# Expert loop of an mLSTM, differential-attention and mixture-of-experts layer: which waits the load queue holds, how tokens beyond 128 are interlaced, and the shape of the mask product

## The chip, the cores and the metric

The kernel runs on one core of one Trainium2 chip. The metric is the device time of one execution in microseconds; the time of a kernel is the median of several executions.

## The reference

One layer over 2048 tokens of width 1024, all in float32. Cut to what matters here:

```python
h = rms_norm(x, norm1_w)
x = x + hybrid_mixer(h, ...)           # mLSTM heads and differential attention, one output projection
h = rms_norm(x, norm2_w)
...
# differential attention: a block of 128 queries sees the keys of its own and earlier chunks of 64
mask = key_chunk[None, :] <= q_chunk[:, None]
p = jax.nn.softmax(jnp.where(mask, s, -jnp.inf), axis=-1)
attn = p[:, :, 0] - lam * p[:, :, 1]
...
# mixture of experts: top 1 of 4 groups, top 2 of its 8 experts, 32 experts in all
hid = jax.nn.silu(xb @ w_gate[e]) * (xb @ w_up[e])     # 1024 -> 512
return hid @ w_down[e]                                 # 512 -> 1024
...
x = x + sum over the 2 experts of weight * expert(h)
```

The routing depends on the inputs. Worked out from the reference with its inputs, 20 of the 32 experts get at most 128 tokens, 6 get 129 to 160, 4 get 161 to 192, and 2 get more (201 and 241).

## The kernel before

The program has four stages, one after the other: the projection of 16 blocks of 128 tokens (to about 320 us of the profiled span), attention and mLSTM for 4 heads (to about 1165 us), output projection with routing (to about 1395 us), and the expert loop (to the end).

**Attention stage.** One loop goes over 64 blocks (head, 128 queries) and writes the atoms of several streams into one order; `score` (L560 on) multiplies queries by keys in float32r, and on the diagonal chunk adds a third product into the same PSUM tile, L577: `qm` by `km`, both bfloat16 with one partition (1 x 128), whose product is -1e30 where the later chunk of 64 is hidden. There are 64 blocks and 2 maps, so 128 mask products.

**Expert loop (L1321).** The places 0 to 32 of the loop run over the experts in an order that the device works out itself: experts 0 and 1 first, then the experts with more than HEAVY tokens (`t3`, L1134) spread evenly between the others, with LEAD moving them earlier or later in their share. For each place:

- The first 128 tokens: gather their rows (`gather`, POOL), transpose and split them into a high and a low part (`turn`), `ffn1` for d = 0..7 (L1227, 6 float32r products of 512 columns for each d), tanh and gating (`hidden`), transpose (`turn_h`, L1232), `ffn2` for f = 0..3 (L1242, 6 products each, one `down(f)`), scale (`emit`, L1247, ACT) and add into the output by a scatter (`scatter`, L1251, POOL). `ffn2` of a place runs in the next place's iteration, and its scatter in the one after that.
- The weights: an expert has 6 raw tiles of 128 x 2048 float32 (1 MiB): 4 with gate and up (L847, two loads of 512 KB), 2 with down (L850). A ring of 12 raw tiles `R` holds two experts. Each half tile is split by ACT (`H`, L66) and DVE (`L`, L70); `ready` puts these splits 6 halves ahead of their use, into the same order as all other work of ACT and DVE.
- Tokens 128 and on (`few`, L1291): if an expert has more than 128, a pass of 32 tokens, if more than 160 a second pass of 32, if more than 192 one of 64. A pass transposes its rows (`few_turn_x`, copy by ACT), multiplies them by the RAW tiles (L1272, then L1287, in plain float32, in column groups of 32 or 64), and writes to `yE`; then one scatter returns all 128 rows of `yE`. So a raw tile is free only when the passes of its expert are over, and the plain path must wait for the branch in any case, as the release stands behind it.

**The load queue.** SP issues everything in the order of the program. In an iteration: `fetch_slots(e + 3)` (L1185: 4 KB of slots into one of 5 buffers `ix`; the buffer is that of place e - 2, whose scatter, issued in this same iteration, must have landed), then behind the branch `done(e - 1, 4)` and `done(e - 1, 5)` (w_down of place e + 1), `done(e, 0)` to `done(e, 3)` (gate and up of place e + 2):

```python
fetch_slots(e + AHEAD)
...
few(e, Q, 0, (lambda: down(2), lambda: down(3)))
with tc.If(n > P + Q, label=f"more{e}b", preferred_fallthrough_block=True):
    few(e, Q, Q)
    with tc.If(n > P + M, label=f"more{e}c", preferred_fallthrough_block=True):
        few(e, M, M)
scatter(yE, IX[e][:, 1])
...
for j in (4, 5):
    done(e - 1, j)
for j in range(4):
    done(e, j)
```

## Time and profile before

| | |
|---|---|
| time, median of 3 runs | 2278.57 us (2271.84 to 2289.45) |
| the profiled execution: time, span | 2281.88 us, 2279.8 us |
| mean granted TensorE clock | 0.969 |
| busy in the span: PE, DVE, ACT, POOL | 92%, 70%, 54%, 23% |
| HBM read and written | 378.51 MB, 87.65 MB |

PE is the matmul engine, DVE VectorE, ACT ScalarE, POOL GpSimd, SP the queue that issues loads. Busy times are those of one profiled execution. Matmuls are pipelined and their ends are modelled, so the distance between the starts of two matmuls says more than the length of one. A wait is put down to the instruction whose semaphore came last.

### The profile page before, as it was taken

The page shows a single profiled execution, that of the slowest core. Times are in us where ns is not written, and L with a number is a line of the kernel's source. Part 1 is how long each engine was busy: PE and PEld are TensorE (multiplying, and loading weights), DVE is VectorE, ACT ScalarE, POOL GpSimd, SP SyncE. Part 2 cuts the span into 40 slices and gives each one's busy share as a digit, 9 for nine tenths or more (in the row PEclk, how much of TensorE's full clock was granted, in tenths as well). Part 3 has the DMA queues.
Part 4 walks back from the last instruction along what each step waited for, and adds up shares of the span by engine and source line. Part 5 has one row for each costly group of instructions (what it writes and reads, how often), then busy time and mean ns, then how long its engine had stood idle before and what let it go on. Part 6 is the DMA issues. An engine that isn't in the chain of part 4 may idle for free. (4 is left out here: it accounts for less than half of the span.)

```text
span 2279.8 us, 40566 instructions
## 1 busy us (share of the span) xinstructions
PE 2099.1 (92%) x13815; PEld 1754.8 (77%) x13816; DVE 1603.2 (70%) x4373; ACT 1230.7 (54%) x2820; POOL 518.5 (23%) x684
## 2 busy tenths in 40 slices
PE   7999989999999999999999996998888999888885
PEld 6888878899999899999877884866666656665664
DVE  6667646886887687788877777876765747666562
ACT  4444324665566566566633334766665656655653
POOL 4000013223322332332111113222232222222312
PEclk9999998999999999999999997999999999999998
DMA  7656368636554663555169442999997859778783
GB/s 220 184 162 188 132 150 226 157 107 163 165 133 116 179 173 105 153 154 145 52 196 302 149 140 92 336 307 303 332 297 257 290 184 317 255 279 269 232 296 48
DMA packets 242336, 452.95 MB, mean 199 GB/s; under 512 B 36368, under 2 KB 120400, under 8 KB 232080
## 3 DMA queue, kind: packets, MB, share of 16 engines
q1 hardware_dynamic: 192160, 316.56, 41.8%
q0 software_dynamic: 49632, 131.86, 22.2%
q8 instruction: 153, 2.51, 0.5%
q10 hardware_dynamic: 272, 1.05, 0.1%
q14 instruction: 119, 0.97, 0.1%
HBM read 378.51 MB, written 87.65 MB: 204 GB/s over the span
## 5 line engine op out<-in xcount | busy, mean ns | idle before, releaser
L70 DVE TENSOR_TENSOR L<-R,H 128x1024 fp32r<-128x1024 f32 x408 | 485.4, 1221 | 184.8 <-ACT H L66 177.7
L66 ACT ACTIVATE H<-R 128x1024 fp32r<-128x1024 f32 x408 | 417.6, 1060 | 154.3 <-DMA R<-w_up 117.9
L1227 PE MATMUL pgu<-H,xT 128*128 128x512 f32 x1024 | 369.1, 418 | 49.7 <-DVE th L1209 28.7
L1227 PEld LDWEIGHTS pgu<-H,xT 128*128 128x128 f32 x1024 | 199.5, 195 | 98.5 <-ACT H L66 28.2
L589 ACT ACTIVATE prob<-sc,nm 128x512 f32<-128x512 f32 (+3 forms) x320 | 196.0, 625 | 51.0 <-DVE nm L586 45.8
L578 DVE TENSOR_REDUCE mx<-sc 128x1 f32<-128x512 f32 (+3 forms) x320 | 187.8, 605 | 35.5 <-PE sc L577 19.4
L1227 PE MATMUL pgu<-L,xT 128*128 128x512 f32 x512 | 207.6, 406 | 0.0
L574 PE MATMUL sc<-kt,qt 128*128 128x512 f32 (+3 forms) x640 | 192.7, 388 | 7.7 <-DMA kt<-k_d 7.2
L1242 PE MATMUL py<-H,hT 128*128 128x512 f32 x512 | 175.4, 405 | 2.1 <-ACT y L1247 1.1
L94 PE MATMUL w<-H,hs 128*128 128x256 f32 x512 | 156.8, 306 | 4.8 <-DVE num L694 4.8
L504 PE MATMUL w<-hs,H 128*128 128x256 f32 x512 | 159.2, 311 | 0.5 <-ACT tho L549 0.5
L633 PE MATMUL w<-va,aT 128*128 128x128 f32 x1088 | 156.3, 277 | 2.2 <-ACT raw L514 1.4
L478 POOL DMA_DIRECT2D qt<-q_d x128 | 78.1, 617 | 299.7 <-DVE g_lf L407 275.4
L633 PEld LDWEIGHTS w<-va,aT 128*128 128x128 f32 x1088 | 139.1, 191 | 8.6 <-ACT raw L514 4.1
L95 PE MATMUL w<-L,hs 128*128 128x256 f32 x512 | 145.8, 285 | 0.0
L96 PE MATMUL w<-H,hs 128*128 128x256 f32 x512 | 145.5, 284 | 0.0
L506 PE MATMUL w<-hs,L 128*128 128x256 f32 x512 | 145.4, 284 | 0.0
L505 PE MATMUL w<-hs,H 128*128 128x256 f32 x512 | 145.3, 284 | 0.0
L1242 PEld LDWEIGHTS py<-H,hT 128*128 128x128 f32 x512 | 97.5, 190 | 31.1 <-issue 7.2
L1251 POOL DMA_INDIRECT out<-y,ix x32 | 58.4, 1825 | 259.8 <-ACT y L1247 166.1
L1227 PEld LDWEIGHTS pgu<-L,xT 128*128 128x128 f32 x512 | 100.3, 196 | 19.8 <-issue 2.3
L1305 POOL TENSOR_SCALAR yE<-yE,ix 32x1024 f32<-32x1024 f32 (+1 forms) x20 | 57.0, 2848 | 253.0 <-ACT yE L1304 130.3
(373 smaller groups left out, 5283.6 us busy)
## 6 DMA issues: line engine op xcount, KB each, us to landing
R<-w_gate SPq DMA_DIRECT2D x128, 512.0 KB, 11.5
R<-w_up SPq DMA_DIRECT2D x128, 512.0 KB, 12.4
R<-w_down SPq DMA_DIRECT2D x63, 1024.0 KB, 8.2
hs<-hT_d POOLq DMA_DIRECT2D x62, 1024.0 KB, 5.4
hT_d<-hs SPq DMA_DIRECT2D x16, 1024.0 KB, 4.1
qt<-q_d POOLq DMA_DIRECT2D x128, 128.0 KB, 6.1
xt<-x SPq DMA_DIRECT2D x30, 512.0 KB, 4.4
q_d<-qkT SPq DMA_DIRECT2D x32, 256.0 KB, 3.7
```

Of the source, the lines that this page charges most:

```text
L66: return A.activation(dst, src, AF.Copy, scale=scale)
L70: return V.tensor_tensor(dst, src, h.bitcast(F32), OP.subtract)
L94: T.matmul(ps, xh, wh, start=start, stop=False)
L95: T.matmul(ps, xh, wl, start=False, stop=False)
L96: T.matmul(ps, xl, wh, start=False, stop=stop)
L504: T.matmul(ps, l0, m0, start=d == 0, stop=False)
L574: T.matmul(ps[:, :n], QT[g // 2][:, o, m, g % 2 * P:(g % 2 + 1) * P], KT[r * 4 + c][:, m, :n], start=o == 0, stop=o == 1 and c < sb)
L578: V.reduce_max(B["mx"][:, m, c:c + 1], ps[:, :n], axis=AX.X)
L589: mark["ACT"] = A.activation(B["p", m][:, c2 * 512:c2 * 512 + n], B["sc", m, c2][:, :n], AF.Exp, bias=nm, scale=0.125, accum_out=B["rs"][: ...
L633: T.matmul(po, B["aT", c][:, kb * P:(kb + 1) * P], VA[r * 4 + c][:, kb, :], start=c == 0 and kb == 0, stop=c == nch - 1 and kb == nb[c] - 1)
L1227: T.matmul(pgu[c], xT[:, l, d, :], r[:, :, n], start=d == 0 and m == 0, stop=d == DC - 1 and m == 2)
L1242: T.matmul(py[n], hT[:, l, f, :], r[:, c], start=f == 0 and m == 0, stop=f == 3 and m == 2)
```

## The change

The two constants of the mask product get 128 partitions, of which only the first is not zero. HEAVY goes from 144 to 128 and LEAD from 0.7 to 0.5. The slot buffers go from 5 to 8. The raw w_down tiles are given back inside the next iteration's `ffn1`, behind the splits of d = 3 and d = 5; the gate and up tiles are given back inside the branch, so that the plain path has a release of its own. `few` is cut into `few_up`, `few_down`, `few_emit` and `few_return`, so that the second pass's rows are turned and its first product runs around the first pass's second product, and the scatter returns 32, 64 or 128 rows. In the last iteration the waiting `emit` stands ahead of `turn_h`. Constants of the routing move from the kernel's start to the output stage.

```diff
-LEAD = 0.7
-HEAVY = 144
+LEAD = 0.5
+HEAVY = 128
...
-        qm = c1.tile([1, P], BF16, name="qm")
+        qm = c1.tile([P, P], BF16, name="qm")
         V.memset(qm, 0.0)
-        V.memset(qm[:, 0:64], NEG)
-        km = c1.tile([1, P], BF16, name="km")
+        V.memset(qm[0:1, 0:64], NEG)
+        km = c1.tile([P, P], BF16, name="km")
         V.memset(km, 0.0)
-        V.memset(km[:, 64:128], 1.0)
+        V.memset(km[0:1, 64:128], 1.0)
...
-                    IX[i] = sp.tile([P, 2, 4], F32, name="ix2", bufs=AHEAD + 2)
+                    IX[i] = sp.tile([P, 2, 4], F32, name="ix2", bufs=AHEAD + 5)
...
-            def few(e, m, r0, between=()):
-
-                between = list(between) + [lambda: None] * 2
-                xH = few_turn_x(m, r0)
-                between[0]()
+            def few_up(e, m, xH, tag=None):
+                return [few_ffn1(xH, e, m, c, tag) for c in range(m // Q)]
+
+            def few_down(e, m, th):
                 hH = sp.tile([P, 2, P], F32, name="hH", bufs=1)
-                th = [few_ffn1(xH, e, m, c) for c in range(m // Q)]
-                between[1]()
                 for c, t in enumerate(th):
                     few_turn_h(t, hH, c)
-                px = few_ffn2(hH, e, m)
+                return few_ffn2(hH, e, m)
+
+            def few_emit(e, m, r0, px):
                 w = D * m // P
                 for q in range(P // m):
                     A.activation(yE[r0:r0 + m, q * w:(q + 1) * w], px[q * m:(q + 1) * m, :w], AF.Copy)
                 G.tensor_scalar(yE[r0:r0 + m], yE[r0:r0 + m], IX[e][r0:r0 + m, 1, 1:2], None, op0=OP.mult)
+
+            def few_return(e, m):
+                scatter(yE[:m], IX[e][:m, 1])
...
+                        if d in (3, 5) and e:
+                            done(e - 1, 4 + d // 4)
...
                 else:
+                    emit(*waiting)
                     hT = new_hT()
                     for d in range(2):
                         turn_h(th[d], hT, d)
-                    emit(*waiting)
...
                     with tc.If(n > P, label=f"more{e}", preferred_fallthrough_block=True) as more:
                         tc.mark_branch_hint_location(f"more{e}b", n > P + Q, engines)
-                        few(e, Q, 0, (lambda: down(2), lambda: down(3)))
-                        with tc.If(n > P + Q, label=f"more{e}b", preferred_fallthrough_block=True):
+                        xH = few_turn_x(Q, 0)
+                        down(2)
+                        ta = few_up(e, Q, xH, "thA")
+                        with tc.If(n > P + Q, label=f"more{e}b", preferred_fallthrough_block=True) as many:
                             tc.mark_branch_hint_location(f"more{e}c", n > P + M, engines)
-                            few(e, Q, Q)
-                            with tc.If(n > P + M, label=f"more{e}c", preferred_fallthrough_block=True):
-                                few(e, M, M)
-                        scatter(yE, IX[e][:, 1])
+                            xH = few_turn_x(Q, Q)
+                            pa = few_down(e, Q, ta)
+                            tb = few_up(e, Q, xH)
+                            few_emit(e, Q, 0, pa)
+                            down(3)
+                            pb = few_down(e, Q, tb)
+                            with tc.If(n > P + M, label=f"more{e}c", preferred_fallthrough_block=True) as most:
+                                xH = few_turn_x(M, M)
+                                few_emit(e, Q, Q, pb)
+                                few_emit(e, M, M, few_down(e, M, few_up(e, M, xH)))
+                                few_return(e, P)
+                            with most.Else():
+                                few_emit(e, Q, Q, pb)
+                                few_return(e, M)
+                        with many.Else():
+                            down(3)
+                            few_emit(e, Q, 0, few_down(e, Q, ta))
+                            few_return(e, Q)
+                        for j in range(4):
+                            done(e, j)
                     with more.Else():
                         down(2)
                         down(3)
+                        for j in range(4):
+                            done(e, j)
...
                 if e:
                     waiting = (py, IX[e - 1][:, 0])
-                    for j in (4, 5):
-                        done(e - 1, j)
                 if e < NE:
-                    for j in range(4):
-                        done(e, j)
                     xT, th = xTn, thn
```

With the counts above, the order of places by their number of further passes (a dot is a plain expert) is

```
before  ....1.11..1...3..3..2...2.12..21
now     ...1.1..1.1..3.3..2.1..1.2..2.2.
```

On SP, in one iteration in the middle of the loop, the kernel before has the slot load with its waits first, then the (empty) branches, then the two loads of w_down (in brackets the semaphores waited for: DMASW are gathers and scatters, DMAHW earlier loads, the others engines):

```order
L1185 DMA ix_19419<-tb_d 128x2x4 [waits DMASW7_49,DMASW5_49,DMAHW5_49,Activation_49,Pool_49]
L1325 TENSOR_LOAD cnti
L1363 COMPARE_AND_BRANCH
L1366 COMPARE_AND_BRANCH
L1369 COMPARE_AND_BRANCH
L1369 UNCONDITIONAL_BRANCH x2
L1366 UNCONDITIONAL_BRANCH
L1363 UNCONDITIONAL_BRANCH x2
L850 ISA
L850 DMA R_15372<-w_down 128x2x1024 [waits DMAHW6_49,DVE_49,PE_49]
L850 ISA
L850 DMA R_15373<-w_down 128x2x1024 [waits DMAHW7_49,DVE_49,PE_49]
```

The same iteration's loads of gate and up follow in the kernel before:

```order
L847 ISA
L847 DMA R_15374<-w_gate 128x2x512 [waits DMAHW0_49,PE_49]
L847 ISA
L847 DMA R_15374<-w_up 128x2x512 [waits DMAHW1_49]
L847 ISA
L847 DMA R_15375<-w_gate 128x2x512 [waits DMAHW2_49,PE_49]
```

On SP in the changed kernel, one iteration from its slot load to its branches:

```order
L1189 DMA ix_19560<-tb_d 128x2x4 [waits DMAHW5_49]
L1331 TENSOR_LOAD cnti
L846 ISA
L846 DMA R_15367<-w_down 128x2x1024 [waits DMAHW6_49,DVE_49,PE_49]
L846 ISA
L846 DMA R_15368<-w_down 128x2x1024 [waits DMAHW7_49,DVE_49,PE_49]
L1371 COMPARE_AND_BRANCH
L1376 COMPARE_AND_BRANCH
L1384 COMPARE_AND_BRANCH
L1384 UNCONDITIONAL_BRANCH x2
L1376 UNCONDITIONAL_BRANCH
```

And in the changed kernel the plain path's loads of gate and up, in the same iteration:

```order
L843 ISA
L843 DMA R_15369<-w_gate 128x2x512 [waits DMAHW0_49]
L843 ISA
L843 DMA R_15369<-w_up 128x2x512 [waits DMAHW1_49]
L843 ISA
L843 DMA R_15370<-w_gate 128x2x512 [waits DMAHW2_49]
```

The slot load has lost its waits for scatters, ACT and POOL; the loads of w_down stand ahead of the branch; and gate and up wait for PE only on the path with further passes.

On PE in the kernel before, from the end of a first further pass to the start of the second (`th`, `hH` belong to the first, `xg` to the second):

```order
L1278 MATMUL pt<-ident,th_21428 128x128 [waits DVE_49,PE_49]
L1287 MATMUL px<-R_15378,hH 32x256 [waits DMAHW7_49,Activation_49]
L1287 MATMUL px<-R_15378,hH 32x256 x7
L1287 MATMUL px<-R_18092,hH 32x256 [waits DMAHW0_49]
L1287 MATMUL px<-R_18092,hH 32x256 x7
L1366 COMPARE_AND_BRANCH
L1367 REGISTER_ALU
L1434 BRANCH_PREFETCH_HINT
L1261 MATMUL pt<-ident,xg_18094 128x32 [waits PE_49]
L1261 MATMUL pt<-ident,xg_18094 128x32 x7
L1272 MATMUL px<-R_15374,xH 32x256 [waits Activation_49]
L1272 MATMUL px<-R_15374,xH 32x256 x7
```

On PE in the changed kernel, the same place:

```order
L1376 COMPARE_AND_BRANCH
L1377 REGISTER_ALU
L1458 BRANCH_PREFETCH_HINT
L1265 MATMUL pt<-ident,xg_18096 128x32 [waits PE_49]
L1265 MATMUL pt<-ident,xg_18096 128x32 x3
L1265 MATMUL pt<-ident,xg_18096 128x32 [waits PE_49]
L1265 MATMUL pt<-ident,xg_18096 128x32 x3
L1282 MATMUL pt<-ident,th_21766 128x128 [waits DVE_49,Activation_49]
L1291 MATMUL px<-R_15373,hH 32x256 [waits DMAHW7_49,Activation_49]
L1291 MATMUL px<-R_15373,hH 32x256 x7
L1291 MATMUL px<-R_18094,hH 32x256 [waits DMAHW0_49]
L1291 MATMUL px<-R_18094,hH 32x256 x7
```

The second pass's transposes and the branch now stand ahead of the first pass's second product, and that product no longer stands between the transposes and the copy that waits for them.

## Rows read from the trace of the kernel before

**Rows 1.** Table by stage: window, length, busy PE PEld DVE ACT POOL, clock, DMA share, GB/s.
```profile
330.00:1165.00 835.00, 818.00 (x6104) 748.86 (x6103) 639.78 (x2058) 490.31 (x1571) 228.22 (x451) 0.99 0.54 145
1400.00:2270.00 870.00, 756.11 (x4758) 559.18 (x4758) 564.71 (x683) 531.61 (x797) 222.95 (x127) 0.95 0.81 266
```

**Rows 2.** Timeline of PE around one mask product: start, us, line, out<-in, shape.
```profile
716.49 0.51 PE L574 MATMUL sc<-kt,qt 128*128 128x384 f32 x2
716.93 0.23 PE L577 MATMUL sc<-km,qm 1*128 1x128 bf16 x1
717.09 0.39 PE L94 MATMUL w<-H,hs 128*128 128x256 f32 x1
717.31 0.28 PE L95 MATMUL w<-L,hs 128*128 128x256 f32 x1
```

**Rows 3.** Timeline of PE around two bfloat16 products of 128 rows, output stage.
```profile
1237.91 0.18 PE L1056 MATMUL prk<-ohb,before 128*128 128x32 bf16 x1
1237.94 0.18 PE L1057 MATMUL prk<-ohb,onesb 128*128 128x32 bf16 x1
1237.96 0.48 PE L94 MATMUL pj<-H,hs 128*128 128x512 f32 x1
1238.28 0.39 PE L95 MATMUL pj<-L,hs 128*128 128x512 f32 x1
1238.51 0.40 PE L96 MATMUL pj<-H,hs 128*128 128x512 f32 x1
```

**Rows 4.** Lines L577 and L1057: weight loads, ns min/median/max.
```profile
L577 PEld LDWEIGHTS <-qm x128: 90/91/98, 345.3 to 1133.9; 1*128 1x128 bf16 x128
...
L1057 PEld LDWEIGHTS <-onesb x16: 96/98/103, 1184.3 to 1389.6; 128*128 128x128 bf16 x16
```

**Rows 5.** Table by expert place, columns as in rows 1.
```profile
1459.40:1477.80 18.40, 18.40 (x86) 14.62 (x85) 16.80 (x20) 12.20 (x17) 6.70 (x4) 1.00 1.03 362
...
1655.40:1673.60 18.20, 18.20 (x85) 14.72 (x86) 15.11 (x19) 15.45 (x22) 8.44 (x4) 1.00 0.84 263
1673.60:1699.90 26.30, 18.71 (x86) 14.35 (x84) 14.12 (x17) 13.32 (x19) 7.57 (x6) 0.93 0.93 288
...
1556.50:1583.90 27.40, 25.02 (x190) 18.04 (x190) 17.93 (x22) 17.75 (x29) 9.33 (x5) 1.00 0.79 238
```

**Rows 6.** Waits of PE from 1400 to 2270: us in total, times, longest us.
```profile
PE pgu L1227 <- DVE th L1209: 28.7, 6, 7.3
PE px L1272 <- ACT xH L1263: 23.6, 11, 7.6
PE pgu L1227 <- PEq L1366: 10.0, 5, 4.1
PE pgu L1227 <- ACT H L66: 7.3, 2, 3.9
```

**Rows 7.** Timeline of SP from 1655 to 1705.
```profile
1678.52 0.38 SPq L1185 DMA_DIRECT2D ix<-tb_d  x1
...
1680.91 0.37 SPq L847 DMA_DIRECT2D R<-w_gate  x1
```

**Rows 8.** Waits of SP from 1400 to 2270.
```profile
SPq L1185 <- DMA out<-y,ix: 209.1, 18, 21.5
```

**Rows 9.** Timeline of ACT from 1660 to 1700.
```profile
1695.48 2.00 ACT L66 ACTIVATE H<-R 128x1024 fp32r<-128x1024 f32 x2 [11.15 <-DMA R<-w_up]
```

**Rows 10.** Timeline of PE, start of a second further pass.
```profile
2134.16 3.66 PE L1272 MATMUL px<-R,xH 128*32 128x256 f32 x64 [1.40 <-ACT xH L1263]
```

**Rows 11.** Timeline at the end: the last scatter.
```profile
2268.29 1.57 POOL L1251 DMA_INDIRECT out<-y,ix  x1 [5.64 <-DMA out<-y,ix]
```

**Rows 12.** Line L1189, gathers: landing; its issue on POOL; the transposes that need it.
```profile
DMA to landing us min/median/max: 3.8/6.9/10.8
...
1469.58 1.76 POOL L1189 DMA_INDIRECT xg<-h_d,ix  x1 [2.21 <-POOLq L1363]
...
1483.79 0.60 PE L1200 MATMUL pt<-ident,xg 128*128 128x128 f32 x4
```

More of the change, by code (lines that the diff above doesn't have):

```diff
@@ L118, in block_kernel @@
         ident = cp.tile([P, P], F32, name="ident")
-        before = cp.tile([P, P], BF16, name="before")
-        onesb = cp.tile([P, P], BF16, name="onesb")
         nw = cp.tile([P, 2], F32, name="nw")
-        cnt = cp.tile([P, NE], F32, name="cnt")
         cnti = cp.tile([1, 3 * NE + 1], I32, name="cnti")
@@ L135, in block_kernel @@
             V.tensor_scalar(ident, jp, 0.0, None, op0=OP.is_equal)
-            V.tensor_scalar(before, jp, 0.0, None, op0=OP.is_gt)
             V.tensor_scalar(cmask, jp, 0.0, NEG, op0=OP.is_lt, op1=OP.mult)
-        V.memset(onesb, 1.0)
-        qm = c1.tile([1, P], BF16, name="qm")
+        qm = c1.tile([P, P], BF16, name="qm")
         V.memset(qm, 0.0)
-        V.memset(qm[:, 0:64], NEG)
-        km = c1.tile([1, P], BF16, name="km")
+        V.memset(qm[0:1, 0:64], NEG)
+        km = c1.tile([P, P], BF16, name="km")
         V.memset(km, 0.0)
-        V.memset(km[:, 64:128], 1.0)
+        V.memset(km[0:1, 64:128], 1.0)
         ones64 = c1.tile([64, P], F32, name="ones64")
@@ L941, in block_kernel @@
             V.memset(ones32, 1.0)
+            cnt = sp.tile([P, NE], F32, name="cnt", bufs=1)
+            onesb = sp.tile([P, P], BF16, name="onesb", bufs=1)
+            V.memset(onesb, 1.0)
+            before = sp.tile([P, P], BF16, name="before", bufs=1)
+            jp = sp.tile([P, P], I32, name="jp", bufs=1)
+            G.iota(jp, pattern=[[1, P]], base=0, channel_multiplier=-1)
+            V.tensor_scalar(before, jp, 0.0, None, op0=OP.is_gt)
             V.memset(cnt, 0.0)
@@ L1203, in turn, with hidden @@
                     split_l(xT[:, 1, h, :], pt, xT[:, 0, h, :])
-            def hidden(pgu, n):
-                th = sp.tile([P, n], F32, name=f"th{n}", tag=f"th{n}")
+            def hidden(pgu, n, tag=None):
+                th = sp.tile([P, n], F32, name=f"th{n}", tag=tag or f"th{n}", bufs=1 if tag else 2)
                 A.activation(th, pgu[:, :n], AF.Tanh, scale=0.5)
@@ L1264, in few_turn_x, with few_ffn1 @@
                 return xH
-            def few_ffn1(xH, e, m, c):
+            def few_ffn1(xH, e, m, c, tag=None):
                 px = pp.tile([P, 512], F32, name="px", bufs=2)
@@ L1273, in few_ffn1 @@
                                  start=d == 0, stop=d == DC - 1, skip_group_check=True)
-                return hidden(px, P)
+                return hidden(px, P, tag)
             def few_turn_h(th, hH, c):
```

## The prediction

> **What bounds the kernel now.** I read the table by stage first, then waits and timelines inside the two stages that the change touches. The attention stage is bound by PE: 818.0 of 835.0 us busy, at clock 0.99, with DVE at 639.8 and the transfers at a share of 0.54 [rows 1]. What shortens PE's own stream there shortens the stage. The expert loop is different: PE is busy for 756.1 of 870.0 us, so 114 us are idle, and the clock is at 0.95 [rows 1]. The table by place shows where: an undisturbed plain expert takes 18.2 to 18.4 us, all of it PE; the one that starts at 1673.6 takes 26.3 with the same 18.7 us of matmul [rows 5].
>
> The waits of PE say what ends the idle time: pgu behind the gating of DVE (28.7 us in 6 waits), the copies of a further pass on ACT (23.6), splits on ACT (7.3) [rows 6]. None of these is slow itself. ACT works in order, and what held it in the 26.3 us place was a split that waited 11.15 us for the tile of w_up, until 1695.48 [rows 9]. Why the tile was late is on SP: in the place that starts at 1655.4 it issued its 4 KB slot load only at 1678.52, 23 us after the place's start, and w_gate, queued behind it, at 1680.91 [rows 7]. The wait in front is the landing of an earlier place's scatter: 209.1 us over 18 places [rows 8]. In that time the engines were free for more: the share was 0.84 [rows 5]. So a 4 KB load that waits for a return stands in front of 6 MB that PE needs soon.
>
> **The change part by part.**
>
> **Weights.** With 8 slot buffers the one that is taken was last used 8 places ago, and its scatter landed long before; the wait goes. What is then next on SP are the splits of w_down at d = 3 and d = 5, some 6 and 10 us into the place (each d is 6 products at 0.23 us [rows 3], and transposes between), and on the plain path nothing more: gate and up have no wait for PE left. So gate and up of the place after next leave about 10 us into a place instead of 25. They are first split at d = 6 of the following place, 10 us into it, so there are about 18 us for a transfer that had 3 (1680.91 to about 1684).
>
> What it is worth: of the waits of PE I count 28.7 + 7.3 [rows 6], and of the 23.6 behind the copies what is over a pass's own 1.40 us [rows 10] in 8 of the 11, so 23.6 - 11.2 = 12.4; together 48.4 us. The lower clock after such stalls adds a little (18.71 against 18.20 us of matmul in the disturbed place, at 0.93 [rows 5]), 50 us in all. Not all of it goes, as the transfers have their own limit: while saturated they moved 362 GB/s [rows 5]; a plain expert needs 6.3 MB of weights and up to 0.5 MB each for gather and return, 7.3 MB, so 20.2 us against 18.2 of PE. Two plain places in a row run 4 us into debt; one with a single pass lasts 27.4 us [rows 5] and pays 7 back. HEAVY = 128 matters here: it puts one of the 12 long places behind every one or two plain ones, where before two had a single pass among plain ones by chance. The smaller returns take 832 of 1536 rows of 4 KB away, 3.4 MB, 9 us of transfer at that rate. I leave 10 us of stalls: -40 us. Bounds: 0, if the transfers are the limit, and -65, if the rest of the 114 us of idle time that comes from ACT's order goes too.
>
> What could be late next is what stands on SP on the path with further passes: gate and up wait there, as before, for the last product that reads the raw tile, some 8 us before the place's end, and are needed 10 us into the next: 18 us again. The slot load of the next place is queued behind them, and is needed only three places later.
>
> **Mask.** Around one mask product, from the first of two 384-column products to the second one after the mask, 0.82 us pass (716.49 to 717.31) [rows 2]. At the regular pace, 0.23 us for 512 columns [rows 3], the two of 384 and the one of 256 take 0.17 + 0.17 + 0.12 = 0.46. So the mask with one row costs 0.36 us, of which its own 128 columns need 0.06; 128 of them are 46 us. The output stage has bfloat16 products with all 128 rows between float32r ones [rows 3]: two of them and one of 512 columns take 0.37 us (1237.91 to 1238.28), so 0.14 for two, 0.07 each with 32 columns; 96 more columns at that pace are 0.04. With 0.11 instead of 0.36 the saving is 0.25 x 128 = 32 us. PE is the bound, but it will meet DVE and ACT more often when it is faster; I take -26. Bounds: 0 and -38 (if only 0.06 is left).
>
> The row shows that the loss is not the weight load: 91 ns with one row and 98 with 128 [rows 4]. The Trainium skill, "TensorEngine Tiling (Array Packing)", Key Properties, says that a change of the tiling mode drains TensorE, which would be such a gap on both sides of a product of 1 row; by it the full 0.25 us go. "TensorE: Matmul & The Clock Gate", Part 3, says that a product of 32 rows takes the same time as one of 128; by that sentence alone the term would be nothing. Side by side, [rows 2, 3] agree with the first.
>
> **Further passes.** A single pass keeps its products; only the branch moves from behind its second product to behind its first. Now PE waits 10.0 us for that branch, 5 times, up to 4.1 [rows 6], with nothing behind it in the queue. Behind `few_up` there are still 64 products to work off, so I expect part of it hidden: -5. With two or three passes, the 1.40 us wait for the copy goes 6 times, but the first pass's gating is then covered only by eight short transposes, and ACT has four writes of yE in front of the second pass's copy; I take -1. Together -6, with bounds -16 (all of the branch and the 6 waits) and +12 (6 places with a branch of 4 us ahead of their second product, less what they pay now).
>
> **End.** The last scatter starts at 2268.29, after 5.64 us behind the landing of the one before [rows 11]. With the waiting `emit` first and a plain expert last, the one before leaves some 6 us earlier: -4 (0 to -5).
>
> The rest costs nothing: the routing constants move to a stage in which POOL and DVE are not the bound (an iota and three small operations of under a microsecond), the wider memsets stand at the start beside the first loads, and SP's new code runs while SP waits anyway; if its jump takes 4 us like PE's longest, 14 us of the 18 are left.
>
> **Sum**, against the profiled execution's own 2281.9 us (3.3 above the median of the runs, well inside their spread): -40 - 26 - 6 - 4 = -76, so 2206 us.
>
> **The rivals.**
>
> *The transfers are the bound.* For it: shares of 1.03 and 0.93 [rows 5], and 20.2 us of transfer for a plain expert. Against it: 0.81 over the whole loop, 0.84 while SP waited, and long places that pay back. Then the stall only moves; I give the weights a third, -13: 2281.9 - 13 - 26 - 6 - 4 = 2233 us.
>
> *The mask gives nothing*, because the gap comes from the change between float32r and bfloat16 and not from the one row, or because DVE and ACT take over at once. The products of [rows 3] speak against the first, PE busy for 0.98 of the stage [rows 1] against the second. 2206 + 26 = 2232 us.
>
> *Gathers come late (slower).* With weights issued 15 us earlier more of them are queued while a gather is under way. A gather issued at 1469.58 is needed at 1483.79, 14.2 us later, and lands after 6.9 us, 10.8 at most [rows 12]. It decides from a landing of 14.2 us on; at 18 us PE loses 3.8 in each of 30 places, 114 us: 2281.9 - 76 + 114 = 2320 us. Against it: 10.8 is the longest although the share was already 1.03 in places. The Trainium skill, "DMA: Bandwidth & Descriptors", section on queues and rings, says that an engine takes its queues in turn, packet by packet, by which a longer queue of weights does not push a gather further back than a busy one; no run here shows that yet, and it is in no number.
>
> *The change doesn't do what it says*: each load also waits for an older load on its own semaphore, so on the plain path SP may be held by landings. That would show as the first rival does.
>
> **How the numbers follow.** Forecast 0.60; a bound by transfers 0.16; no gain from the mask 0.13; more than I count (the upper bounds of weights and passes, near 2175) 0.07; gathers late 0.04. The range 2166 to 2256 reaches 40 us below the forecast, about what the far bounds of weights and mask add (25 + 12), and 50 above it, which takes in the two middle rivals with some 20 us to spare; outside are the slow one and tails. A measurement of this kernel tells about 1% from no change, so 2256 is the border of faster. The forecast lies 50 us below it and the two middle rivals 23: of their 0.29 I put 0.07 above the border, and of the forecast 0.03. Faster 0.86, same 0.10, slower 0.04.
>
> **What would show it.** Right: L577's starts 0.1 us apart from their neighbours and an attention stage some 26 us shorter; slot loads that follow the last w_up at once; w_gate issued about 10 us into plain places; ACT's wait for w_up far below its present sum; plain places near 18.3 us throughout. Wrong: plain places of over 22 us with a share near 1.0 (transfers), an attention stage of the same length (mask), transposes of xg that wait for DMA (gathers), or single-pass places of over 30 us (branch).

## The result and the profile after

| | before | after |
|---|---|---|
| time, median of 4 runs | 2284.0 us (2271.8 to 2292.0) | 2193.2 us (2190.1 to 2200.5) |
| the profiled execution's span | 2279.8 us | 2198.6 us |
| mean granted TensorE clock | 0.969 | 0.981 |

The changed kernel takes 0.961 of the time before, with an interval of 0.956 to 0.967: 91 us less by the medians. The forecast was 76 less, 2206 us, and the result lies in its range. As the account at the end shows, the sum was nearer than its terms.

The first two rows below are the kernel before, the next two the changed one, in the table by stage (columns as in [rows 1]). The windows begin and end at the same instructions in both kernels: the attention stage from its first score product to its last mask product, the expert loop from the first product of `ffn1` to the end.

```profile
344.67:1133.90 789.23, 781.13 (x5883) 716.80 (x5883) 616.93 (x1992) 474.20 (x1532) 218.55 (x426) 0.99 0.53 145
1405.06:2279.80 874.74, 754.28 (x4751) 557.60 (x4750) 559.94 (x678) 528.47 (x793) 221.03 (x126) 0.95 0.80 264
```

```profile
341.56:1118.76 777.20, 757.84 (x5883) 706.92 (x5884) 614.06 (x1992) 472.29 (x1531) 219.05 (x426) 1.00 0.55 148
1387.83:2198.60 810.77, 732.52 (x4751) 553.33 (x4750) 561.15 (x678) 528.68 (x793) 226.45 (x126) 0.97 0.83 280
...
1854.37:1872.27 17.90, 17.90 (x84) 14.73 (x85) 15.22 (x19) 16.61 (x23) 9.94 (x6) 1.00 1.01 347
```

The attention stage is 12.0 us shorter, not 26: PE's busy time falls by 23.3 us, and its idle time (length less busy) rises from 8.1 to 19.4. The loop is 64.0 us shorter, against 50 forecast for weights, passes and end: its idle time falls from 120.5 to 78.3 us, and its busy time by 21.8. The last row is a plain place in the middle: 17.90 us, all of it PE, at a share of 1.01. Before, the shortest were 18.2 [rows 5]; nothing in the forecast makes a place shorter than that. Stage and loop together are 76 of the 81 us between the two profiled spans; the other 5 lie in the projection and in the output stage, where the forecast has no term.

The timeline of SP in the changed kernel, in the place that starts at 1854.37, answers to [rows 7]:

```profile
1857.26 0.58 SPq L843 DMA_DIRECT2D R<-w_up  x1
1858.73 0.38 SPq L1189 DMA_DIRECT2D ix<-tb_d  x1
1862.67 3.23 SPq L846 DMA_DIRECT2D R<-w_down  x2
1866.56 0.37 SPq L843 DMA_DIRECT2D R<-w_gate  x1
```

The slot load follows the last w_up at once, and the first w_gate leaves 12.2 us into the place (forecast: about 10; before: 25). The waits in the loop (us in total, times, longest), ACT's for w_up in the kernel before, then in the changed one, then PE's two longest in the changed one, are:

```profile
ACT H L66 <- DMA R<-w_up: 117.9, 44, 11.2
```

```profile
ACT H L66 <- DMA R<-w_up: 8.5, 6, 2.3
```

```profile
PE pt L1204 <- DMA xg<-h_d,ix: 16.5, 7, 7.0
PE px L1291 <- ACT hH L1283: 16.5, 18, 4.2
```

Weights are hardly waited for any more. A new wait stands first: transposes that wait for a gather. One of its 7 is the loop's first gather (7.0 us), which the kernel before pays too (6.9); the other 6 (9.5 us) it had not at all. The second row, the wait of a pass's second product for its turned rows, grew from 7.0 us in 18 before (longest 0.4); experiment 6 comes back to it.

The timeline of PE around one mask product answers to [rows 2]:

```profile
708.18 0.51 PE L570 MATMUL sc<-kt,qt 128*128 128x384 f32 x2
708.53 0.23 PE L573 MATMUL sc<-km,qm 128*128 128x128 bf16 x1
708.57 0.36 PE L94 MATMUL w<-H,hs 128*128 128x256 f32 x1
708.77 0.28 PE L95 MATMUL w<-L,hs 128*128 128x256 f32 x1
```

From the first of the 384-column products to the second one behind the mask 0.59 us pass, where it was 0.82. Over all 128 masks this distance falls by 0.21 us on average, 27 us in all; the step had 0.25 each, 32 us. Of the 0.36 us that the step read for one mask that leaves 0.15.

The end, in the timeline of the changed kernel:

```profile
2184.49 0.39 PE L1246 MATMUL py<-H,hT 128*128 128x512 f32 x1
2187.14 1.56 POOL L1255 DMA_INDIRECT out<-y,ix  x1 [5.99 <-DMA out<-y,ix]
```

The last return still waits 6 us for the one before [rows 11], but from the last product's start to the end of the span 14.1 us pass, where it was 18.4 (2261.4 to 2279.8).

### The profile page after: what moved, and what is told of

The parts are those of the page before. It is cut to its first block, busy times and chain, and to the rows that moved or that the text cites. A ratio compares the mean times of both kernels' runs of the same rounds, so it can differ in the third digit from the quotient of the medians.

```text
span 2198.6 us, 40400 instructions
## 1 busy us (share of the span) xinstructions
PE 2050.7 (93%) x13815; PEld 1737.1 (79%) x13816; DVE 1604.1 (73%) x4373; ACT 1229.0 (56%) x2820; POOL 524.6 (24%) x685
## 5 line engine op out<-in xcount | busy, mean ns | idle before, releaser
L1231 PE MATMUL pgu<-H,xT 128*128 128x512 f32 x1024 | 361.8, 411 | 17.8 <-issue 6.9
L574 DVE TENSOR_REDUCE mx<-sc 128x1 f32<-128x512 f32 (+3 forms) x320 | 187.3, 604 | 29.8 <-PE sc L570 14.2
L1246 PEld LDWEIGHTS py<-H,hT 128*128 128x128 f32 x512 | 97.4, 190 | 35.5 <-issue 14.2
L1193 POOL DMA_INDIRECT xg<-h_d,ix x64 | 90.3, 1410 | 128.9 <-PE py L1246 46.0
L570 PEld LDWEIGHTS sc<-kt,qt 128*128 128x128 f32 x640 | 100.5, 192 | 16.2 <-ACT prob L585 7.4
## 6 DMA issues: line engine op xcount, KB each, us to landing
R<-w_down SPq DMA_DIRECT2D x63, 1024.0 KB, 10.3
```

Source lines behind the costliest of these rows:

```text
L570: T.matmul(ps[:, :n], QT[g // 2][:, o, m, g % 2 * P:(g % 2 + 1) * P], KT[r * 4 + c][:, m, :n], start=o == 0, stop=o == 1 and c < sb)
L574: V.reduce_max(B["mx"][:, m, c:c + 1], ps[:, :n], axis=AX.X)
L1231: T.matmul(pgu[c], xT[:, l, d, :], r[:, :, n], start=d == 0 and m == 0, stop=d == DC - 1 and m == 2)
L1246: T.matmul(py[n], hT[:, l, f, :], r[:, c], start=f == 0 and m == 0, stop=f == 3 and m == 2)
```

## The experiments

Each was timed in 4 to 10 runs beside the kernel before on the same chip (medians of before: 2281.8 to 2284.8). "Run 3" below is the experiment of that number. First four that ask where the gain is made.

**1. The start of xT and hT.** Three more slot buffers of 32 bytes move what is allocated behind them by 96 bytes. In the kernel before, `xT` and `hT`, the stationary operands of the expert products, start 32 bytes beyond a multiple of 64 (xT at 194400 in the built program); in the changed one at a multiple of 64 (193856; the constants that went elsewhere account for 640 bytes, ten times 64). To see if this is why a plain place became shorter, a tile that nothing uses was put ahead of the slot buffers, in the changed kernel and, alone, in the kernel before. It also moves the tiles of `th` and `y` and the operands of the passes; of what the products of 512 columns read, it moves only xT and hT:

```diff
             yE = sp.tile([P, D], F32, name="yE", bufs=1)
+            pad = sp.tile([P, 8], F32, name="pad", bufs=1)
-            for t in (xg0, xg1, yE):
+            for t in (xg0, xg1, yE, pad):
```

> The changed kernel with one unused tile of 32 bytes ahead of the slot buffers, so that xT and hT (the stationary operands of both expert products) start 32 bytes beyond a multiple of 64, as they did before, instead of at one. Theory A (the start addresses set the pace of the expert products): the distance of two 512-column products goes from 0.227 back to 0.232 us, the shortest plain place from 17.9 to 18.2 us, and with 2304 such products the expert loop and the time get 10 to 12 us longer, about 2204. Theory B (the pace came from somewhere else in the change, fewer waits on PE or less traffic): pace 0.227, plain place 17.9, time 2193 as the changed kernel.

> The kernel before with the same tile of 32 bytes, which puts xT and hT at a multiple of 64; nothing else. Theory A: pace 0.227 us, plain place 17.9, the expert loop 8 to 11 us shorter, about 2273. Theory B: pace 0.232, plain place 18.2, no change, 2284.

Measured: 2201.0 us (ratio to before 0.965, 0.962 to 0.967) and 2283.2 us (1.001, 0.999 to 1.003). A plain place of the first, then of the second, in the table by stage:

```profile
1714.52:1732.73 18.21, 18.21 (x87) 14.77 (x86) 15.17 (x19) 17.30 (x23) 10.31 (x6) 1.00 0.94 289
```

```profile
1762.36:1780.33 17.97, 17.97 (x87) 14.76 (x85) 14.89 (x19) 17.05 (x23) 10.99 (x6) 1.00 0.67 167
```

The pace follows the address in both directions, so theory A holds for the place: 0.3 us. It fails for the time. In the kernel before the 0.3 us are worth nothing, which would follow if its places wait for weights anyway; in the changed kernel the shift costs 3 to 8 us by the medians (it was timed twice, 2193.2 and 2197.6), but the intervals overlap and the profiled loop, 808.0 us, lies between the 805.0 and 810.8 of the changed kernel's two. No cost in time is shown.

**2. The mask alone.** The kernel before with the two constants of 128 rows:

```diff
-        qm = c1.tile([1, P], BF16, name="qm")
+        qm = c1.tile([P, P], BF16, name="qm")
...
-        km = c1.tile([1, P], BF16, name="km")
+        km = c1.tile([P, P], BF16, name="km")
```

> The kernel before with the mask product of 128 rows alone. The prediction's step: 26 us off the attention stage, 2258. Rival, read from the trace of the changed kernel: the products around the mask save 20 us or more by their distances, but other products wait longer, and the stage gets only 12 us shorter, 2272. The loop behind it keeps its length (875 us from its first product) in both.

Measured: 2269.4 us, ratio 0.995 (0.993 to 0.997). That is 12 us by the ratio, 15 by the medians. The attention stage in its table by stage:

```profile
342.85:1123.88 781.03, 760.67 (x5883) 709.92 (x5884) 613.27 (x1992) 473.22 (x1531) 219.84 (x426) 0.99 0.54 147
```

Busy 20.5 us less, idle 12.3 us more (20.4 instead of 8.1), so 8.2 us shorter; the loop behind it keeps its 874.7 us. The rest of the 14.5 us between the two profiled spans lies in the projection and in the output stage, where this edit has nothing to gain, so the mask is worth 8 us by its stage and 12 to 15 by the time. The rival is right. What PE waits for in the stage is spread thin; the longest waits of this kernel there are:

```profile
PE w L94 <- DVE num L694: 6.8, 3, 3.2
PE sc L574 <- DMA kt<-k_d: 5.6, 1, 5.6
PE w L633 <- ACT raw L514: 4.4, 11, 0.5
PE w L504 <- ACT tho L549: 2.9, 4, 0.8
```

Before, the same four were 4.8, 7.2, 1.4 and 0.5.

**3. The slot buffers alone.** The kernel before with `bufs=AHEAD + 4` in place of `AHEAD + 2`, nothing else:

> The kernel before with 7 slot buffers instead of 5 (7, not 8, so that xT and hT keep their place against a multiple of 64); no release is moved. The prediction's step: the slot load's wait for a return was what made the weights late, so most of the 40 us of the weights term comes with it alone, 25 to 35 us, about 2254. Rival: the releases behind the branch hold SP as long as the slot load did (the weights of the next place follow them in order), so it gives less than 10 us and only the moved releases give the rest.

Measured: 2240.0 us, ratio 0.981 (0.978 to 0.985): 43 to 45 us, more than the step's 25 to 35. Its loop in the table by stage, and two of its waits, PE's and ACT's:

```profile
1407.92:2239.98 832.06, 742.67 (x4751) 552.61 (x4750) 561.08 (x678) 531.52 (x793) 223.62 (x126) 0.97 0.82 277
```

```profile
PE pt L1200 <- DMA xg<-h_d,ix: 23.8, 8, 6.9
...
ACT H L66 <- DMA R<-w_up: 28.3, 18, 3.2
```

The loop is 42.7 us shorter: 31.1 us of idle time, 11.6 of busy time (the clock is at 0.97, not 0.95). ACT waits 28 us for w_up where it was 117.9. And the wait for gathers appears, 23.8 us in 8, where the kernel before had only the first one of 6.9.

Then four runs that take one part out of the changed kernel. It ran beside the first three; the fourth ran on another chip. First the changed kernel itself:

> The changed kernel itself, once more, beside the runs below on the same chip: 2193 us, expert loop 803 to 811 us.

Measured: 2197.6 us (0.963, 0.961 to 0.966); its profiled loop lasts 805.0 us.

**4. Releases behind the branch again**, all six:

```diff
-                        if d in (3, 5) and e:
-                            done(e - 1, 4 + d // 4)
...
                     waiting = (py, IX[e - 1][:, 0])
+                    for j in (4, 5):
+                        done(e - 1, j)
+                if e < NE:
+                    for j in range(4):
+                        done(e, j)
```

> The changed kernel with all releases behind the branch again, as before: w_down of place e - 1 and gate and up of place e follow the branch, in this order. Theory A (the prediction: with the slot load out of the way the transfers have time to spare, and a release 10 us later is still early enough): within 5 us of the changed kernel, and plain places that follow each other keep about 18 us. Theory B (the earlier release carries part of the weights term): 10 to 20 us longer, with plain places of 20 to 25 us behind other plain ones and waits of ACT for w_up of 30 us or more in sum.

Measured: 2192.2 us (0.959, 0.957 to 0.962), 5 us less than the changed kernel, with intervals that overlap. No part of the gain is seen to come from the earlier releases: theory A.

**5. The old order of places**, HEAVY = 144 and LEAD = 0.7:

> The changed kernel with HEAVY = 144 and LEAD = 0.7 again, so that two places with a single pass stand among plain ones by chance. Theory A (the prediction: transfers run into debt in long rows of plain places, so the order matters): 5 to 10 us longer, with plain places of over 20 us where three or more stand in a row. Theory B (with the slot load gone the transfers keep up in any order): within 4 us.

Measured: 2192.6 us (0.960, 0.958 to 0.963), again 5 us less with overlapping intervals. Theory B, as it is not longer: ACT waits for w_up 27.3 us in 17 instead of 4.4 in 5, and the time does not show it.

**6. The passes one after the other, returns of 128 rows.** `few` and the branch as before, releases as in the changed kernel:

```diff
-                        xH = few_turn_x(Q, 0)
-                        down(2)
-                        ta = few_up(e, Q, xH, "thA")
...
+                        few(e, Q, 0, (lambda: down(2), lambda: down(3)))
...
+                        scatter(yE, IX[e][:, 1])
```

> The changed kernel with the further passes one after the other as before, and returns of 128 rows; the releases stay in the branch. Theory A (the prediction: the passes are worth 6 us, and the smaller returns some more): 6 to 12 us longer than the changed kernel, places with two passes 38 us instead of 35, with three 51 instead of 48, with one 27 to 28 instead of 27. Theory B (the passes were shorter only because weights came earlier): within 4 us of the changed kernel and places with two passes at 35 to 36.

Measured: 2223.7 us (0.975, 0.972 to 0.977), 26 us longer: more than theory A gives. Some 3 of them lie outside the profiled span (4.8 to 5.4 us of each execution do so here, 1.7 to 1.9 in the changed kernel), and no row shows why. A place with two passes lasts 37.4 to 42.6 us where the changed kernel has 34.4 to 38.1. The timeline of PE in such a place, from the first pass's second product on:

```profile
1852.13 1.93 PE L1291 MATMUL px<-R,hH 128*32 128x256 f32 x32 [0.37 <-ACT hH L1283]
1853.99 0.68 PE L1265 MATMUL pt<-ident,xg 32*128 32x32 f32 x8
1856.07 3.66 PE L1276 MATMUL px<-R,xH 128*32 128x256 f32 x64 [1.40 <-ACT xH L1267]
1860.87 0.30 PE L1282 MATMUL pt<-ident,th 128*128 128x128 f32 x1 [1.13 <-DVEq L1375]
1861.59 1.93 PE L1291 MATMUL px<-R,hH 128*32 128x256 f32 x32 [0.43 <-ACT hH L1283]
```

The same in the changed kernel (the second run of it):

```profile
1836.45 0.68 PE L1265 MATMUL pt<-ident,xg 32*128 32x32 f32 x8
1837.65 0.30 PE L1282 MATMUL pt<-ident,th 128*128 128x128 f32 x1 [0.52 <-DVE th L1213]
1838.32 1.93 PE L1291 MATMUL px<-R,hH 128*32 128x256 f32 x32 [0.37 <-ACT hH L1283]
1840.07 3.64 PE L1276 MATMUL px<-R,xH 128*32 128x256 f32 x64
...
1846.78 1.93 PE L1291 MATMUL px<-R,hH 128*32 128x256 f32 x32 [1.37 <-ACT hH L1283]
```

The bracketed waits are 3.33 us there and 2.26 here, as small as the step had them. In the whole loop the wait for the copies of `xH` goes from 12.0 us to 0.4, and the wait for those of `hH` rises from 7.0 to 16.0. Summed over all 12 places with passes, from the last product of `ffn1` to the next place's first, PE is idle for 46.7 us with the old passes and 39.7 with the new ones. The six places with one pass gain nothing: they last 164.3 us together with the old passes and 168.1 in the changed kernel. Seven of the 26 us are explained; the next run looks for the rest in the returns.

**7. Returns of 128 rows, interlaced passes.**

```diff
-                scatter(yE[:m], IX[e][:m, 1])
+                scatter(yE, IX[e][:, 1])
```

> The changed kernel with interlaced passes, but each return scatters all 128 rows again. Undoing both cost 26 us, while PE's own idle time at the passes explains 7. Theory A (the returns are the rest: 3.4 MB of them stand ahead of the gathers, and the transposes of xg wait): 12 to 18 us longer than the changed kernel, waits of PE for xg of 15 us or more in sum where the changed kernel has 8. Theory B (the rest is the order of the passes, which also moves splits and emits): within 4 us.

Measured: 2217.0 us (0.969, 0.964 to 0.974). The changed kernel did not run beside it, so its two measurements elsewhere bound the difference: 13 to 17 us longer by the ratios to the kernel before, 19 to 24 by the medians, and 13.5 to 19.3 by the profiled loops. That is theory A, and theory B is out. PE's wait for xg in the loop:

```profile
PE pt L1204 <- DMA xg<-h_d,ix: 28.7, 10, 7.1
```

Without the loop's first gather that is 21.6 us in 9, where the changed kernel has 8.1 to 9.5 in 6. POOL's timeline behind a place with one pass shows how; first with 128 rows, then in the changed kernel (second run) with 32:

```profile
1590.87 2.02 POOL L1255 DMA_INDIRECT out<-yE,ix  x1 [0.28 <-POOL yE L1308]
1593.19 1.07 POOL L1193 DMA_INDIRECT xg<-h_d,ix  x1 [0.30 <-issue]
1601.20 1.60 POOL L1255 DMA_INDIRECT out<-y,ix  x1 [6.94 <-ACT H L66]
1603.11 1.85 POOL L1193 DMA_INDIRECT xg<-h_d,ix  x1 [0.30 <-PE py L1246]
```

```profile
1582.36 1.79 POOL L1255 DMA_INDIRECT out<-yE,ix  x1 [0.28 <-POOL yE L1308]
1584.46 1.08 POOL L1193 DMA_INDIRECT xg<-h_d,ix  x1 [0.30 <-issue]
1589.14 1.60 POOL L1255 DMA_INDIRECT out<-y,ix  x1 [3.60 <-ACT H L66]
1591.05 1.54 POOL L1193 DMA_INDIRECT xg<-h_d,ix  x1 [0.30 <-PE py L1246]
```

In each group the first row is the return of the pass and the third the return of a place's 128 rows. Both add into the same output, and the second leaves 10.3 us after the first, or 6.8 with 32 rows; and the gather of a later place (last row) stands behind it on POOL, issued 12.2 us after the first return, or 8.7. PE's transposes then waited in the slower kernel:

```profile
1613.44 1.09 PE L1204 MATMUL pt<-ident,xg 128*128 128x128 f32 x4 [3.67 <-DMA xg<-h_d,ix]
```

What the second return waits for is the landing of the first, not ACT, whose name the third row gives. The copies of ACT that make its `y` had ended at 1592.2 in the slower kernel, 9 us before it left. The first return's time from issue to landing, with 128 rows, then with 32:

```profile
1590.96 1.26 ACT L1251 ACTIVATE y<-py,ix 128x512 f32<-128x512 f32 x2
...
DMA to landing us min/median/max: 9.5/9.5/9.5
```

```profile
DMA to landing us min/median/max: 5.9/5.9/5.9
```

In both kernels the second return leaves 0.8 us behind that landing, and so it does in 10 of the 11 pairs of this kind whose landing each trace tells. Against the second run of the changed kernel the loop is 19.3 us longer: 10 are idle time (86.1 instead of 75.8) and 9 are busy time at a lower clock, as its row and that of the changed kernel show (against the first run it is 8 and 6):

```profile
1393.45:2217.73 824.28, 738.20 (x4751) 557.66 (x4750) 562.55 (x678) 528.93 (x793) 220.01 (x126) 0.96 0.83 280
```

```profile
1385.89:2190.88 804.99, 729.21 (x4751) 550.88 (x4750) 561.25 (x679) 529.00 (x793) 227.97 (x126) 0.98 0.83 282
```

Three more runs on what was left open.

**8. No mask at all.** The changed kernel without L573:

```diff
-                             start=o == 0, stop=o == 1 and c < sb)
-                if c == sb:
-                    T.matmul(ps[:, n - P:n], qm, km, start=False, stop=True)
+                             start=o == 0, stop=o == 1)
```

> The changed kernel without the mask products, so that a query also sees the later chunk of its own block. By their distances they still cost 0.15 us each, 19 us in all. Theory A (what is saved at the masks is given back, because PE meets ACT and DVE): under 8 us off the attention stage, and PE's waits there grow. Theory B (PE alone sets the stage, and the mask's rest costs less than its distances say or all of it): 15 to 19 us off, with PE's idle time unchanged.

Measured: 2198.9 us (0.961, 0.957 to 0.966). From its first to its last score product the stage lasts 775.5 us, where the changed kernel has 777.0 and 777.4:

```profile
343.60:1119.10 775.50, 749.13 (x5757) 708.69 (x5758) 613.98 (x1992) 473.64 (x1529) 216.75 (x426) 0.99 0.54 148
```

Busy 8.7 us less than after, idle 26.4 instead of 19.4. Theory A: PE alone no longer sets the stage.

**9. The same alignment for hs0**, the stationary operand of the projection and the output stage:

```diff
-        hs0 = keep.__enter__().tile([P, 2, 2, DC, P], F32R, name="hs0")
+        kp = keep.__enter__()
+        hs0 = kp.tile([P, 2, 2, DC, P], F32R, name="hs0")
+        kpad = kp.tile([P, 8], F32, name="kpad")
...
+        cpad = c1.tile([P, 8], F32, name="cpad")
```

The second tile, `cpad`, fills up what lies below, so that the tiles there keep their place against a multiple of 64.

> The changed kernel with 32 unused bytes behind the operand hs0, which is the stationary one of the projection and of the output stage and starts 32 bytes beyond a multiple of 64: now it starts at one. Theory A (what the first run shows for xT and hT holds for any stationary operand): the 768 and 738 products of 512 columns of the two stages go from 0.232 to 0.227 us, and the 768 of 260 columns lose half as much: 3.8 + 3.7 + 1.9, about 9 us, as these stages are bound by PE, 2186 us beside 2195. Theory B (the pace of these products has another reason): no change of the pace, 2195.

Measured: 2202.0 us (0.962, 0.957 to 0.967), and the median distance of 512-column products is 0.232 to 0.233 us in the projection, as without it. Theory A falls: that a multiple of 64 helps is seen for xT and hT in the loop, and is no rule for stationary operands. Why it does there stays open.

**10. The gather ahead of the return.** An attempt to beat both kernels:

```diff
                         if d == 2 and waiting:
-                            emit(*waiting)
+                            sent = emit(*waiting, send=e + 2 >= NE)
...
                                 gather(IX[e + 2][:, 0], xg0)
+                                if waiting:
+                                    scatter(*sent)
```

> The changed kernel with the return of a place's first 128 rows issued behind the gather of d = 5 instead of ahead of it (at d = 2); the copies of ACT stay at d = 2. Theory A (what is left of the waits for xg comes from returns that stand ahead of a gather in POOL's queue): PE's waits for xg fall from 8 to 16 us in sum to under 3, and the time by 5 to 10 us, 2185 to 2190. Theory B (the return now comes later and collides with what follows it, or the waits have another reason): within 4 us of 2195, or slower.

Measured: 2191.6 us (0.960, 0.957 to 0.963): no faster than the changed kernel. The wait went as theory A says, down to the loop's first gather; the time did not. PE's waits in this kernel's loop:

```profile
PE py L1246 <- issue: 11.8, 4, 3.3
PE pgu L1231 <- issue: 8.8, 3, 5.3
PE pt L1204 <- DMA xg<-h_d,ix: 7.6, 1, 7.6
```

The first of them, behind the branch in a place with one pass, was 6.1 us in 4 after the change. The six such places take 178.8 us together where the changed kernel has 168.1 to 170.6, and these 8 to 11 us eat what the plain places win.

## Why the prediction was right, and by which steps it was not

The time fell as forecast, and half of it for the reason named first. That the sum came so near is luck in part: the loop gave 64.0 us where the forecast had 50, the attention stage 12.0 where it had 26, and the two misses cancel. The terms by one run each, by the time where nothing else is said:

| step | forecast | shown by | measured |
|---|---|---|---|
| the slot load's wait | in the -40 | run 3 | -43 to -45 |
| earlier releases, order of places | in the -40 | runs 4, 5 | nothing |
| smaller returns and further passes | in the -40, and -6 | run 6 | -26 |
| of these, smaller returns | in the -40, as 9 us of transfer | run 7 | -13 to -24 |
| mask | -26 | run 2 | -8 (stage) to -15 |
| end | -4 | traces | -4 |
| pace of plain places | not seen | run 1 | 0 to -8 |

They add up to 81 to 98 us; 91 and 86 were measured for the whole change in two comparisons. The further passes alone are what the returns leave of the 26, 2 to 13 us; 7 us of PE's idle time are theirs by the traces.

**Weights: the cause right, the size too small.** The step read 209.1 us of waiting on SP [rows 8] as what made the split of w_up late [rows 9], and changing the number of buffers alone shows it. Two things about it were wrong. The forecast gave the releases and HEAVY = 128 a share, because transfers would run into debt at 20.2 us for a plain place; but the changed kernel has places of 17.9 us at a share of 1.01 between longer ones, and each of the two parts can be undone alone for nothing. And the clock was sized too small. Of PE's waits that the step counted (48.4 us) run 3 takes 40.8 away (28.7 to 2.1, 7.3 to 4.0, 23.6 to 12.7), close to the 38 that it expected, and waits for gathers take 16.9 back; but 11.6 us of busy time go at the higher clock, where the step had 2. The fourth rival, loads that wait for the landing of older ones, hardly shows: the loads of gate and up wait 15.3 us in 18 for landings in the changed kernel's loop.

**Returns: priced as a transfer, worth more than that as a wait.** The step counted 3.4 MB at 362 GB/s, 9 us of a resource, and 13 to 24 were measured. What they cost is order: a return that lands later holds the next return, and that one the gather behind it on POOL. That is the third rival (gathers come late), at a seventh of its price of 114 us: run 3 shows it appear once weights come early (23.8 us of waits, 16.9 without the first), and run 7 shows the smaller returns taking more than half of it back. The chain explains 12 to 14 us of waits (21.6 instead of 8.1 to 9.5); that the rest of the 13 to 24 is the clock behind them is likely, not shown. The rival looked at the wrong quantity: it decided from a landing of 14.2 us on, but gathers in the changed kernel land after 8.0 us (median) and 11.6 at most; it is their issue that comes late. "DMA: Bandwidth & Descriptors", queues and rings, in the Trainium skill has the engines take queues in turn by packet; the traces agree as far as they go. With the weights issued early the median landing of a gather goes from 6.9 [rows 12] to 8.0 us only, and in run 10 it is 8.0 as well while the waits vanish, because there the gather is ahead of the return in POOL's own order.

**Mask: the mechanism right, the term about double.** A mask costs 0.21 us less (27 us in all; the step had 0.25, 32). The miss is what is given back: 6 us were allowed for PE meeting DVE and ACT more often, and of the 27 us the stage kept 12.0 in the whole change and 8.2 in run 2, so 15 to 19 were lost. The step argued from PE busy for 0.98 of the stage [rows 1] that PE would stay the bound; run 8 shows that it did not: with the masks gone altogether (19 us by the 0.15 that is left of each) the stage gains 1.5 to 1.9 us. The rival that the gap comes from the change of type and not from the one row is out for the larger part: the type stayed, and 0.21 of 0.36 us went; what the remaining 0.09 beyond the product's own 0.06 is stays open. The product itself is recorded at 0.23 us with one row and with 128, which speaks for a loss around it, as the step had it. This agrees with the Trainium skill, "TensorEngine Tiling (Array Packing)", Key Properties, on a drained TensorE at a change of the tiling mode; the price here is 0.21 us for one such product. The Trainium skill's sentence on 32 rows stands in "TensorE: Matmul & The Clock Gate" under "Why this matters for your kernels", not in Part 3; the 0.23 us of the product itself agree with it.

**Passes and end** came near what was worked out: 7 us of idle time for the passes (2 to 13 by the time), and 4 us for the end. Part of the first is a trade: PE no longer waits at the end of single-pass places but in their middle, behind the branch (6.1 us in 4), and the wait for `xH` became one for `hH`, as the step expected in part.

**The signs that it named** held but for two: slot loads leave at once, w_gate early, and ACT's wait for w_up is at 8.5 us; but the attention stage is 12 us shorter and not 26, and of 17 plain places, at 17.9 us where they are not disturbed, 5 still last over 20. One sign of being wrong, transposes of xg that wait for DMA, did show, at 9.5 us.

## What to carry to other kernels

Look in a load queue for the small load that waits for something slow: what it costs is what stands behind it, and here two more buffers were worth more than any reordering of the large loads. Price a transfer by who waits behind it, not only by its bytes. Do not take a gain on an engine that is busy for 98% of a stage at its full size: here more than half of it was given back. A term is known only when it is run alone: here two errors of 14 us cancelled.

## What the runs showed that was not expected

- The start address of their stationary operands changes the pace of the expert products: 18.2 us a place when xT and hT start 32 bytes beyond a multiple of 64, 17.9 to 18.0 when they start at one, in both kernels and both directions (run 1); for hs0 in other stages it makes no difference (run 9), and the cause is open. Adding slot buffers of 32 bytes changed it by accident.
- Taking away a wait of 8 us (run 10) or undoing a part that saves 23 us of ACT's waits (run 5) leaves the time as it was: of the idle time that is left in the loop (78 us of PE's), neither of these two waits is worth its length.
